# A plain fp32 query projection, early picks of two heads, and gate products one step later, in a one-core encoder layer with expert retrieval

## The chip, the cores and the metric

The kernel runs on one core of one Trainium2 chip. The metric is the device time in microseconds (us), the median of several runs. Names of engines: PE is TensorE (PEld its weight loads), DVE VectorE, ACT ScalarE, POOL GpSimd, SP the engine that issues most transfers.

## What is computed

One encoder layer for two sequences of 256 tokens (`x_prompt` and `x_sample`), width 1024: normalisation, input projection, a gated short convolution beside grouped-query attention, output projection, and then an expert retrieval in place of a feed-forward part. Only that last part matters here:

```python
q = (xf @ wq).reshape(T, 8, 2, 128)                  # 8 heads, two halves of 128
s = einsum('thpc,hpnc->thpn', q, subkeys)            # 128 key scores for each half
sv, si = top_k(s, 16)
cand = sv[..., 0, :, None] + sv[..., 1, None, :]     # 16 x 16 sums
cv, cp = top_k(cand, 16)
eidx = take_along_axis(si[0]*128 + si[1], cp)        # 16 experts of 16384, for each head
gates = softmax(cv)
a = gelu(einsum('thkd,td->thk', u_tab[eidx], x)) * gates
out = einsum('thk,thkd->td', a, v_tab[eidx])
```

## The kernel before

**Two ways to the experts.** The prompt's two tiles of 128 tokens *gather*: for each of 8 x 16 = 128 picks of a tile one indirect DMA from POOL (`g_issue`, L159) fetches one row of `uv` for each token, 128 rows of 8 KB, about 1 MB (`grow`); DVE forms the dot with `xg` (`g_dot`, L185), ACT the gelu and the gate (`g_weight`), DVE adds the weighted second half to `hg` (`g_val`). That is 256 gathers, through a ring of four tiles (`GBUF`, pool `ga`). The sample goes *densely*: every key row j of `u` (512 KB) is multiplied with all 256 tokens (the S loop, 128 steps, `pSj`, L880), times a dense gate matrix A, and A is then multiplied with every row of `v` (the V loop, 128 steps, `acc`, L908). A comes from one-hot matrices: for four tokens at a time `gates_dense` (L804) has DVE and ACT make `oi`, `oj`, `gh`, `gl` and PE multiply them (`pgm`, L855 and L856, eight products in fp16), 64 such steps.

**Order of the work.** The program is written in one stream, and a scheduler then orders each engine's instructions. First `front(0)` (prompt), then `projections` for the prompt (L742: eight heads in two halves each, `pqq`, and the key scores, `pn`), then the picks of tile 0 (`step0` while the heads go by; `fin0`, that is gates and decoding, after the last), `front(1)` (sample), `projections` for the sample, the S loop, the V loop. Work beside these is paced by credits: `bg(us)` after a piece of PE work adds `us` times a share to two accounts; whenever account a holds `GU` = 2.65, `gather()` handles one gather, and account b pays for steps of the tasks (tile 1's picks, later `gates_dense`). Picks enter `queue` when they are decoded; here all 128 of tile 0 after the last head (L753). In the V loop the gathers that are left are spread over 126 steps (L911). A gather's issue also waits for the PE instruction before it in the program (`pe_mark`), for its ring slot and for its index.

**Precision.** The prompt's projections run in a split form: `weights(..., split)` (L111) has ACT and DVE cut each weight tile into `whi` and `wlo` (in two tiles of the same ring `ga` as the gathers), `norm_T` cuts the activations (`xr` and `xrl`), and `mm` (L126) multiplies three terms in fp32r. The sample's run in plain fp32, where one call of the program is two PE instructions in the trace.

**Buffers.** Weights and `u`, `v` tiles go through four tiles of 512 KB (`wp`; the V loop has two more), loaded by SP. The S loop has four PSUM tiles for `pSj`, each freed by DVE's product with A (L885).

Of the kernel before, what the change touches and what calls it, by code (L numbers as in the profile page):

```python
# [18 lines left out]
P = 128  # L19
# [16 lines left out]
JH = 94  # L36
SF = 0.5
# [9 lines left out]
def encoder_layer(ctx: ExitStack, tc: tile.TileContext, xp, xs_, meta, vec, w_in, w_out, wq,  # L47
# [186 lines left out]
    def retrieval(pools, sv, si, cv, cp, gs, scores, t0, lkbuf, dc):  # L234
# [31 lines left out]
        def gates(t):  # L266
            ge_ = gate_all[:, t0 + t].rearrange("p (h k) -> p h k", k=KTOP)
            dve.tensor_tensor(ge_, cv[:, t], cv[:, t, :, 0:1].to_broadcast([P, PH, KTOP]), op=ALU.subtract)
            act.activation(gate_all[:, t0 + t], gate_all[:, t0 + t], AF.Exp)
            dve.tensor_reduce(gs[:, t], ge_, axis=AX.X, op=ALU.add)  # L270
            dve.reciprocal(gs[:, t], gs[:, t])
            dve.tensor_tensor(ge_, ge_, gs[:, t, :, None].to_broadcast([P, PH, KTOP]), op=ALU.mult)

        def lookup(mask, tab2, out):
            w = lkbuf(0)
            if tab2 is None:
                dve.tensor_tensor(w.rearrange("p h a k -> p h (a k)"), mask.rearrange("p h a k -> p h (a k)"),
                                  dc[:, 1:2].rearrange("p o a k -> p o (a k)").to_broadcast([P, PH, 256]), op=ALU.mult)
            else:
                dve.tensor_tensor(w.rearrange("p h a (k r) -> p (h a) k r", r=2),  # L280
                                  mask.rearrange("p h a (k r) -> p (h a) k r", r=2),
                                  tab2.rearrange("p h a r -> p (h a) r")[:, :, None, :].to_broadcast([P, PH * 16, 8, 2]),
                                  op=ALU.mult)
# [6 lines left out]
        def decode(t):  # L290
            s16 = t2.tile([P, 16, KTOP], F16, tag="s16", name="s16", bufs=1)
            dve.tensor_copy(s16, si[:, t])
            c16 = t2.tile([P, PH, KTOP], F16, tag="c16", name="c16", bufs=1)
            dve.tensor_copy(c16, cp[:, t])
            s4 = s16.rearrange("p (h q) k -> p h q k", q=2)
            di = t2.tile([P, PH, KTOP, 2], F16, tag="di", name="di", bufs=1)
            dj = t2.tile([P, PH, KTOP, 2], F16, tag="dj", name="dj", bufs=1)
            for r in range(2):
# [3 lines left out]
            mk = lkbuf(1)  # L302
            dve.tensor_tensor(mk, c16[:, :, None, :].to_broadcast([P, PH, 16, 16]),
                              dc[:, 0:1].to_broadcast([P, PH, 16, 16]), op=ALU.is_ge)
            lookup(mk, di, idx_i[:, t].rearrange("p (h k) -> p h k", k=KTOP))
            yield 6.0
            b16 = t2.tile([P, PH, KTOP], F16, tag="b16", name="b16", bufs=1)
            lookup(mk, None, b16)
            dve.tensor_tensor(b16, c16, b16, op=ALU.subtract)
            yield 4.0  # L310
            mk2 = lkbuf(1)
            dve.tensor_tensor(mk2, b16[:, :, None, :].to_broadcast([P, PH, 16, 16]),
                              dc[:, 2:3].to_broadcast([P, PH, 16, 16]), op=ALU.is_equal)
            lookup(mk2, dj, idx_j[:, t].rearrange("p (h k) -> p h k", k=KTOP))
            if t0 == 0:
                dve.scalar_tensor_tensor(eidx[:, t], idx_i[:, t], 128.0, idx_j[:, t], op0=ALU.mult, op1=ALU.add)
            yield 5.0
# [8 lines left out]
        def all_steps(tiles):  # L326
            for hd in range(PH):
                yield from head_steps(hd, tiles)
            for t in tiles:
                yield from fin_steps(t)  # L330

        def fin_steps(t):
            gates(t)
            yield 1.0
            yield from decode(t)

        return head_steps, fin_steps, all_steps

    def projections(xr, sk, scores, qp, step=None, split=False):
# [84 lines left out]
    def front(s, h):  # L424
# [275 lines left out]
        for t in range(2):  # L700
            tok = slice(t * P, (t + 1) * P)
            norm_T(lambda c: xr[:, c, tok], xs2[t], (lambda c: xrl[c.start // 4][:, :, tok]) if sp else None)
# [10 lines left out]
        if sp:  # L713
            return lambda c, k: xrl[c // 4][:, c % 4] if k else xr[:, c]
# [21 lines left out]
    heads0, fin0, _ = retrieval(r0t, *picks(r0p, "p0"), sc0, 0, lk0, dc0)  # L736
# [16 lines left out]
    queue.extend((0, k) for k in range(P))  # L753
# [33 lines left out]
    heads1, fin1, _ = retrieval(q1, *pk1, sc1, 2, lk1, dc1)  # L787
# [14 lines left out]
    tau = [0]  # L802

    def gates_dense():  # L804
# [13 lines left out]
        for t in range(2):  # L818
# [14 lines left out]
            yield 1.6  # L833
            for o in range(P // OC):
# [16 lines left out]
                for q in range(OC // 4):  # L851
                    pg = psg.tile([P, 4, P], F32, tag="g", name="pgm")
                    for r in range(4):
                        k = 4 * q + r
# [135 lines left out]
```

## Time and profile before

| | us |
|---|---|
| median of 3 runs | 1413.37 (1413.35 to 1417.03) |
| the profiled execution's own time | 1417.84 |
| its span | 1415.9 |
| PE, DVE, ACT, POOL busy | 94%, 72%, 33%, 31% of the span |

| stretch of the profiled span | us |
|---|---|
| `front(0)` | 0 to 143 |
| prompt's projections | 143 to 196 |
| `front(1)` | 196 to 345 |
| sample's projections | 345 to 416 |
| S loop | 416 to 950 |
| V loop | 950 to 1412 |

The profiled execution took 4.5 us more than the median; the span leaves out 1.9 us around it. Busy shares are averages over stretches with different limits, and a busy PE is not a PE at its peak, so the rows further down are taken by stretch.

### The profile page before, as it was taken

Reading aid. Unit: us, or ns where it says so; the run is one execution under the profiler, and the core shown is the slowest. Engines: PE = TensorE matmul, PEld = TensorE weight load, DVE = VectorE, ACT = ScalarE, POOL = GpSimd, SP = SyncE. Lnnn points to the kernel's source line nnn. Section 1 sums busy time; section 2 is a strip of 40 time slices with the busy share of each in tenths; the row PEclk is TensorE's granted clock in tenths of the full one; section 3 lists DMA queues with packets and bytes.
Section 4 is the critical chain, followed back from the end, with each engine's and each line's share of the span. In section 5 each row is a group of like instructions: output and inputs, shape, how many; then the busy total and the mean of one; then the engine's idle time right before and its main releaser. Section 6 shows DMA issues by size and latency. Waiting matters only on the chain. (4 is left out here: it accounts for less than half of the span.)

```text
span 1415.9 us, 17764 instructions
## 1 busy us (share of the span) xinstructions
PE 1329.3 (94%) x5868; PEld 925.7 (65%) x5868; DVE 1026.0 (72%) x2307; ACT 470.2 (33%) x1577; POOL 445.1 (31%) x481
## 2 busy tenths in 40 slices
PE   6998998998989987999999999899999999999998
PEld 5887996677868875788787787674433333344443
DVE  5656899775998876877887777576666666665665
ACT  4554433632222225777776311111111111111110
POOL 2101124331433221112121234243545545423331
PEclk9999999999999998999999999999999999999999
DMA  6434537578979997888988999899999999999997
GB/s 209 135 120 141 174 104 276 191 261 298 346 271 345 399 353 253 324 297 315 328 327 291 360 418 418 351 399 417 415 417 417 418 416 417 417 416 416 416 417 298
DMA packets 90235, 460.20 MB, mean 325 GB/s; under 512 B 10512, under 2 KB 11024, under 8 KB 57120
## 3 DMA queue, kind: packets, MB, share of 16 engines
q0 software_dynamic: 37296, 270.02, 48.2%
q1 hardware_dynamic: 50832, 182.33, 35.0%
q10 hardware_dynamic: 2016, 6.72, 1.3%
q8 instruction: 46, 0.75, 0.2%
q14 instruction: 45, 0.37, 0.1%
HBM read 454.81 MB, written 4.19 MB: 324 GB/s over the span
## 5 line engine op out<-in xcount | busy, mean ns | idle before, releaser
L159 POOL DMA_INDIRECT grow<-in_uv,eidx x256 | 366.3, 1431 | 701.4 <-DMA grow<-in_uv,eidx 174.0
L132 PE MATMUL pSj<-xr,u 128*128 128x256 f32 x2048 | 492.2, 392 | 21.0 <-DVE Ah L64 13.1
L132 PEld LDWEIGHTS pSj<-xr,u 128*128 128x128 f32 x2048 | 375.5, 193 | 85.3 <-DVE Ah L64 19.3
L64 DVE SCALAR_TENSOR_TENSOR grow<-grow,xg 128x1024 f32<-128x1024 f32 x256 | 312.7, 1222 | 158.1 <-DMA grow<-in_uv,eidx 150.4
L64 DVE SCALAR_TENSOR_TENSOR hg<-grow,aw,hg 128x1024 f32<-128x1024 f32 x256 | 328.4, 1283 | 89.7 <-ACT aw L64 88.2
L908 PE MATMUL acc<-v,Al 128*128 128x512 f32 x752 | 340.1, 601 | 4.9
L908 PEld LDWEIGHTS acc<-v,Al 128*128 128x128 f32 x752 | 137.3, 190 | 207.1 <-issue 146.1
L64 ACT ACTIVATE dots<-dots 128x1 f32<-128x1 f32 x256 | 51.6, 202 | 636.1 <-DVE grow L64 635.9
L908 PE MATMUL acc<-v,Ah 128*128 128x512 f32 x272 | 116.9, 592 | 0.0
L64 ACT ACTIVATE gl<-oj,gf 128x128 f16<-128x128 f16 x256 | 95.5, 393 | 9.7 <-DVE oj L64 9.4
L908 PEld LDWEIGHTS acc<-v,Ah 128*128 128x128 f32 x272 | 51.7, 190 | 65.1 <-issue 64.8
L64 ACT ACTIVATE aw<-dots,gate_all 128x1 f32<-128x1 f32 x256 | 74.8, 293 | 6.8
L64 DVE TENSOR_TENSOR wlo<-w,whi 128x1024 fp32r<-128x1024 f32 x42 | 51.1, 1218 | 19.2 <-ACT whi L64 13.2
L64 ACT ACTIVATE gh<-oj,gf 128x128 f16<-128x128 f16 x128 | 50.5, 394 | 27.5 <-DVE oj L64 27.2
L64 DVE TENSOR_TENSOR oj<-dup,io 128x512 f16<-128x512 f16 x64 | 27.1, 424 | 44.6 <-ACT gl L64 44.4
L132 PE MATMUL pqq<-xr,w 128*128 128x256 f32 x256 | 59.1, 385 | 0.0
L855 PE MATMUL pgm<-gh,oi 128*128 128x128 f16 x256 | 47.6, 220 | 11.3 <-ACT gh L64 11.3
L132 PEld LDWEIGHTS pqq<-xr,w 128*128 128x128 f32 x256 | 48.4, 194 | 6.4 <-ACT xr L64 0.2
L64 ACT ACTIVATE whi<-w 128x1024 fp32r<-128x1024 f32 x42 | 44.0, 1056 | 23.0 <-PE pqq L132 11.9
L856 PE MATMUL pgm<-gl,oi 128*128 128x128 f16 x256 | 49.0, 220 | 0.1
L132 PE MATMUL pc<-xT,w 128*128 128x258 f32 (+1 forms) x192 | 47.5, 390 | 1.1 <-DVE rb L64 0.6
L132 PEld LDWEIGHTS pc<-xT,w 128*128 128x128 f32 x192 | 34.9, 192 | 8.6 <-issue 2.5
(261 smaller groups left out, 1568.6 us busy)
## 6 DMA issues: line engine op xcount, KB each, us to landing
u<-in_u_t SPq DMA_DIRECT2D x128, 512.0 KB
v<-in_v_n SPq DMA_DIRECT2D x128, 512.0 KB
w<-in_w_in SPq DMA_DIRECT2D x36, 512.0 KB
w<-in_wq SPq DMA_DIRECT2D x32, 512.0 KB
w<-in_w_out SPq DMA_DIRECT2D x16, 512.0 KB
grow<-in_uv,eidx POOLq DMA_INDIRECT x256, 10.3
hdram<-h ACTq DMA_DIRECT2D x3, 512.0 KB
h<-in_xp SPq DMA_DIRECT2D x2, 512.0 KB
```

The source lines that it names most:

```text
L64: i = f(*a, **k)
L132: i = pe.matmul(out, st_(c, a), mv(c, b), start=(n == 0), stop=(n == NC * len(terms) - 1))
L159: i = pool.indirect_dma_start(out=r, out_offset=None, in_=uv, in_offset=bass.IndirectOffsetOnAxis(ap=eidx[:, t, k:k + 1], axis=0))
L855: pe.matmul(pg[:, r, :], oi[:, k, :], gh[:, k, :], start=True, stop=False)
L856: pe.matmul(pg[:, r, :], oi[:, k, :], gl[:, k, :], start=False, stop=True)
L908: i = pe.matmul(acc[t][q], A(j)[:, t * P:(t + 1) * P], vb[:, q * 512:(q + 1) * 512], start=j == 0, stop=j == P - 1, skip_group_check=True)
```

## The change

Three edits. `projections` of the prompt loses its split form: `w` is used as loaded, `xr` is fp32, `xrl` is gone. Decoding takes a range of heads, and `step0` decodes and queues the picks of heads 0 and 1 as soon as head 1 is chosen, the other six after head 7; from then on account a grows with the share `S0`. And `gates_dense` hands a step's products to `gate_unit` one step later.

```diff
+HPART = (2, PH)
+S0 = 0.4
...
-        def gates(t):
+        def gates(t, ha, hb):
...
-        def decode(t):
+        def decode(t, ha, hb):
+            n_h = hb - ha
...
+            mk = lkbuf(1)[:, :n_h]
...
             if t0 == 0:
-                dve.scalar_tensor_tensor(eidx[:, t], idx_i[:, t], 128.0, idx_j[:, t], op0=ALU.mult, op1=ALU.add)
+                dve.scalar_tensor_tensor(eidx[:, t, ks], idx_i[:, t, ks], 128.0, idx_j[:, t, ks], op0=ALU.mult, op1=ALU.add)
...
-            w = weights(wq, hd, split)
+            w = weights(wq, hd)
...
-                mm(pq, lambda c, k: w(c, k)[:, pp * P:(pp + 1) * P], xr, split=split)
+                mm(pq, lambda c, k: w(c)[:, pp * P:(pp + 1) * P], xr)
...
-        xr = gc.tile([P, NC, 256], F32R if sp else F32, tag="xr", name="xr")
-        if sp:
-            xrl = [r0t.tile([P, 4, 256], F32R, tag=f"lk{i}", name=f"xrl{i}", bufs=1) for i in range(2)]
+        xr = gc.tile([P, NC, 256], F32, tag="xr", name="xr")
...
     def step0(hd):
         for _ in heads0(hd, [0]):
             pass
-
-    projections(xr0, sk0, sc0, r0t, step0, True)
-    for _ in fin0(0):
-        pass
+        if hd + 1 in HPART:
+            ha = ([0] + list(HPART))[HPART.index(hd + 1)]
+            for _ in fin0(0, ha, hd + 1):
+                pass
+            if not ha:
+                credit["a"] = 0.0
+                share["a"] = S0
+            queue.extend((0, k) for k in range(ha * KTOP, (hd + 1) * KTOP))
+
+    projections(xr0, sk0, sc0, r0t, step0)
...
     tasks.append(tile1())
-    queue.extend((0, k) for k in range(P))
     share.update(a=SF, b=SB0)
...
+    def gate_unit(oi, gh, gl, a):
+        pg = psg.tile([P, 4, P], F32, tag="g", name="pgm")
+        for r in range(4):
+            pe.matmul(pg[:, r, :], oi[:, r, :], gh[:, r, :], start=True, stop=False)
+            pe.matmul(pg[:, r, :], oi[:, r, :], gl[:, r, :], start=False, stop=True)
...
+        tau[0] = a + 4
...
-                tau[0] = t * P + s0 + OC
+                due.append((oi, gh, gl, t * P + s0))
+                if len(due) > 1:
+                    gate_unit(*due.pop(0))
                 yield 1.1 + (4 * r_done[0] + 60) / 700
+            gate_unit(*due.pop(0))
```

POOL's queue at the first gathers (`cd` are the candidate sums of a head, `qst` belongs to `front`). Before:

```order
L258 TENSOR_TENSOR cd<-p0sv 128x3
L259 TENSOR_TENSOR cd<-p0sv 128x6
L106 TENSOR_TENSOR qst<-qst,mhalf 128x2 x2
L159 DMA grow<-in_uv,eidx 128x2048 x4
L106 TENSOR_TENSOR qst<-qst,mhalf 128x4 x2
```

After the change:

```order
L261 TENSOR_TENSOR cd<-p0sv 128x6
L264 TENSOR_TENSOR cd<-p0sv 128x8
L161 DMA grow<-in_uv,eidx 128x2048 x4
L260 TENSOR_TENSOR cd<-p0sv 128x16 x2
L260 TENSOR_TENSOR cd<-p0sv 128x8
```

The first four gathers stand among the candidate sums of the prompt's heads instead of behind `front(1)`'s first norms. Counted over the whole queue, 36 gathers stood before the first PE instruction of the S loop, 115 were tied to S steps and 105 to V steps; now it is 43, 116 and 97.

PE's queue at the first gate products, behind the three transposes that open `gates_dense`. Before:

```order
L823 MATMUL pg<-ident,gate_all 128x128
L132 MATMUL pSj<-xr,u 128x256 x11
L855 LDWEIGHTS oi
L855 MATMUL pgm<-gh,oi 128x128
L856 LDWEIGHTS oi
L856 MATMUL pgm<-gl,oi 128x128
L132 MATMUL pSj<-xr,u 128x256
L855 LDWEIGHTS oi
L855 MATMUL pgm<-gh,oi 128x128
```

After the change:

```order
L841 MATMUL pg<-ident,gate_all 128x128
L134 MATMUL pSj<-xr,u 128x256 x16
L809 LDWEIGHTS oi
L809 MATMUL pgm<-gh,oi 128x128
L810 LDWEIGHTS oi
L810 MATMUL pgm<-gl,oi 128x128
L809 LDWEIGHTS oi
L809 MATMUL pgm<-gh,oi 128x128
```

16 calls of the S loop stand ahead of the first product instead of 11, and the eight products of the step follow each other. Over the whole queue the 512 products stood in 222 unbroken runs between `pSj` calls, and now stand in 166.

ACT's queue in the prompt's projections (`qs` frees PE's PSUM tile of a half head). Before:

```order
L64 ACTIVATE qs<-pqq 128x256
L64 ACTIVATE sc_1571<-pn 128x256
L64 ACTIVATE whi<-w 128x1024
L64 ACTIVATE qs<-pqq 128x256
L64 ACTIVATE sc_1571<-pn 128x256
```

After the change, at the twelfth half head:

```order
L66 ACTIVATE sc_1565<-pn 128x256
L66 ACT_TABLE_LOAD
L66 ACTIVATE dots<-dots 128x1 x2
L66 ACTIVATE aw<-dots,gate_all 128x1 x2
L66 ACTIVATE qs<-pqq 128x256
```

The weight cuts are gone, and gelus of early gathers stand ahead of the copies that free PE's tiles.

## Rows read from the trace of the kernel before

**Rows 1.** The chain of work that ended last, pieces in order of time: start us, length us, what.
```profile
932.63 17.84 PE pSj L132 x80
950.47 44.65 PE acc L908 x104
...
1016.13 18.91 DMA v<-in_v_n
...
1267.60 144.48 PE acc L908 x336
```

**Rows 2.** Busy time by stretch: the stretch and its length, then for PE, PEld, DVE, ACT, POOL busy us and (x instructions), the granted clock, the DMA engines' share, GB/s.
```profile
143.00:196.30 53.30, 53.30 (x444) 53.27 (x444) 47.15 (x225) 24.61 (x46) 9.45 (x51) 0.97 0.50 153
196.30:345.00 148.70, 131.77 (x643) 104.05 (x642) 121.02 (x408) 59.52 (x156) 51.98 (x100) 0.97 0.67 240
...
545.60:800.00 254.40, 251.91 (x1472) 203.85 (x1470) 199.27 (x415) 178.71 (x715) 51.51 (x46) 1.00 0.86 310
800.00:950.20 150.20, 134.54 (x588) 112.39 (x587) 104.43 (x148) 27.32 (x108) 57.06 (x40) 0.97 0.97 393
950.20:1267.50 317.30, 312.44 (x690) 125.15 (x688) 209.06 (x251) 42.05 (x169) 147.85 (x82) 1.00 1.02 416
```

**Rows 3.** The same view for the gather tiles on POOL alone: busy us and (x gathers issued), then granted clock, DMA share, GB/s.
```profile
196.30:345.00 148.70, 23.59 (x20) 0.97 0.67 240
345.00:416.00 71.00, 13.66 (x12) 0.98 0.86 315
416.00:545.60 129.60, 32.81 (x27) 0.92 0.89 341
545.60:800.00 254.40, 51.51 (x46) 1.00 0.86 310
800.00:950.20 150.20, 55.33 (x37) 0.97 0.97 393
950.20:1267.50 317.30, 147.85 (x82) 1.00 1.02 416
```

**Rows 4.** The same view for the V loop's products (`acc`) on PE alone; eight instructions are one step.
```profile
950.20:1267.50 317.30, 312.33 (x688) 1.00 1.02 416
1267.50:1412.00 144.50, 144.43 (x337) 1.00 0.96 393
```

**Rows 5.** DMA queues from 1000 to 1200 us: packets, MB, share of the 16 engines (q0 carries POOL's transfers, q1 SP's); and the transfers issued.
```profile
q0 software_dynamic: 7607, 55.41, 66.9%
q1 hardware_dynamic: 7637, 27.81, 34.8%
...
v<-in_v_n SPq DMA_DIRECT2D x53, 512.0 KB
grow<-in_uv,eidx POOLq DMA_INDIRECT x53, 11.2
```

**Rows 6.** PE in order of time (start us, length us): the key scores after two following half heads in the prompt's projections (split), and a half head with the scores around it in the sample's (plain).
```profile
156.71 0.61 PE L346 MATMUL pn<-sk,qs 128*128 128x128 f32 x4
...
159.99 0.61 PE L346 MATMUL pn<-sk,qs 128*128 128x128 f32 x4
...
356.87 0.61 PE L346 MATMUL pn<-Ah,qs 128*128 128x128 f32 x4
357.31 3.62 PE L132 MATMUL pqq<-xr,w 128*128 128x256 f32 x16
360.77 0.61 PE L346 MATMUL pn<-Ah,qs 128*128 128x128 f32 x4
```

**Rows 7.** DVE in order of time ahead of the prompt's projections, and PE's first product there.
```profile
137.26 1.22 DVE L64 TENSOR_TENSOR wlo<-w,whi 128x1024 fp32r<-128x1024 f32 x1
...
139.13 0.68 DVE L64 TENSOR_TENSOR xrl<-pt,xr 128x512 fp32r<-128x512 f32 x1
139.88 1.28 DVE L64 SCALAR_TENSOR_TENSOR xs<-h,sst,gf 128x1024 f32<-128x1024 f32 x1
...
143.02 1.01 PE L132 MATMUL pqq<-xr,whi 128*128 128x256 f32 x3
143.82 0.50 PE L132 MATMUL pqq<-xrl,whi 128*128 128x256 f32 x1
```

**Rows 8.** PE in order of time around the first gate product, and further on in the gate steps (idle before, and what ended it, in brackets).
```profile
523.44 4.91 PE L132 MATMUL pSj<-xr,u 128*128 128x256 f32 x22
539.68 0.26 PE L855 MATMUL pgm<-gh,oi 128*128 128x128 f16 x1 [11.33 <-ACT gh L64]
...
645.14 0.65 PE L132 MATMUL pSj<-xr,u 128*128 128x256 f32 x2
645.63 0.22 PE L856 MATMUL pgm<-gl,oi 128*128 128x128 f16 x1
645.69 0.65 PE L132 MATMUL pSj<-xr,u 128*128 128x256 f32 x2
```

**Rows 9.** DVE in order of time at the same place.
```profile
536.09 1.22 DVE L64 SCALAR_TENSOR_TENSOR grow<-grow,xg 128x1024 f32<-128x1024 f32 x1 [2.19 <-DMA grow<-in_uv,eidx]
...
538.44 0.42 DVE L64 TENSOR_TENSOR oi<-dup,io 128x512 f16<-128x512 f16 x1
```

**Rows 10.** Waits: who waited for what, us in total, times, longest us. DVE from 143 to 345 us, PE from 345 to 416 us.
```profile
DVE grow L64 <- DMA grow<-in_uv,eidx: 11.0, 8, 3.0
...
PE pn L346 <- ACT qs L64: 6.7, 3, 4.7
```

More of the change, by code (lines that the diff above doesn't have):

```diff
@@ L288, in lookup @@
             dve.tensor_tensor(out, w[:, :, 0, :], w[:, :, 1, :], op=ALU.add)
[L290 to L294 removed]
+        def decode(t, ha, hb):
+            n_h = hb - ha
+            s16 = t2.tile([P, 16, KTOP], F16, tag="s16", name="s16", bufs=1)[:, :2 * n_h]
+            dve.tensor_copy(s16, si[:, t, 2 * ha:2 * hb])
+            c16 = t2.tile([P, PH, KTOP], F16, tag="c16", name="c16", bufs=1)[:, :n_h]
+            dve.tensor_copy(c16, cp[:, t, ha:hb])
             s4 = s16.rearrange("p (h q) k -> p h q k", q=2)
[L296 to L297 removed]
+            di = t2.tile([P, PH, KTOP, 2], F16, tag="di", name="di", bufs=1)[:, :n_h]
+            dj = t2.tile([P, PH, KTOP, 2], F16, tag="dj", name="dj", bufs=1)[:, :n_h]
             for r in range(2):
@@ L324, in head_steps, with fin_steps, projections @@
             yield 0.5 + 1.5 * len(tiles)
[L326 to L333, printed above, removed]
+        def fin_steps(t, ha=0, hb=PH):
+            gates(t, ha, hb)
             yield 1.0
-            yield from decode(t)
-        return head_steps, fin_steps, all_steps
-    def projections(xr, sk, scores, qp, step=None, split=False):
+            yield from decode(t, ha, hb)
+        return head_steps, fin_steps
+    def projections(xr, sk, scores, qp, step=None):
         late = []
@@ L701, in front @@
             tok = slice(t * P, (t + 1) * P)
-            norm_T(lambda c: xr[:, c, tok], xs2[t], (lambda c: xrl[c.start // 4][:, :, tok]) if sp else None)
+            norm_T(lambda c: xr[:, c, tok], xs2[t])
         hold[0] = False
@@ L734, in lk0 @@
         return r0t.tile([P, PH, 16, 16], F16, tag=f"lk{i}", name=f"lk{i}", bufs=1)
-    heads0, fin0, _ = retrieval(r0t, *picks(r0p, "p0"), sc0, 0, lk0, dc0)
+    heads0, fin0 = retrieval(r0t, *picks(r0p, "p0"), sc0, 0, lk0, dc0)
     def step0(hd):
@@ L802, in encoder_layer @@
     tau = [0]
+    def gate_unit(oi, gh, gl, a):
[3 more added lines that the diff above has]
+            pe.matmul(pg[:, r, :], oi[:, r, :], gl[:, r, :], start=False, stop=True)
+        n = r_done[0]
+        pj = pg.rearrange("p t j -> p j t")
+        for part, lo, hi in ((Al, 0, JH), (Ah, JH, P)):
+            m = min(max(n, lo), hi)
+            if m > lo:
+                av = part[:, 0:m - lo, a:a + 4]
+                dve.scalar_tensor_tensor(av, pj[:, lo:m], 1.0 / GSH, av, op0=ALU.mult, op1=ALU.mult)
+            if m < hi:
+                act.activation(part[:, m - lo:hi - lo, a:a + 4], pj[:, m:hi], AF.Copy, scale=1.0 / GSH)
+        tau[0] = a + 4
     def gates_dense():
@@ L833, in gates_dense @@
             yield 1.6
+            due = []
             for o in range(P // OC):
@@ L850, in gates_dense @@
                     act.activation(gl[:, q, :], oj[:, q, :], AF.Copy, scale=gf2[:, 1, s0 + q:s0 + q + 1])
[L851 to L854, printed above, removed]
-                        pe.matmul(pg[:, r, :], oi[:, k, :], gh[:, k, :], start=True, stop=False)
-                        pe.matmul(pg[:, r, :], oi[:, k, :], gl[:, k, :], start=False, stop=True)
-                    a = t * P + s0 + 4 * q
-                    n = r_done[0]
-                    pj = pg.rearrange("p t j -> p j t")
-                    for part, lo, hi in ((Al, 0, JH), (Ah, JH, P)):
-                        m = min(max(n, lo), hi)
-                        if m > lo:
-                            av = part[:, 0:m - lo, a:a + 4]
-                            dve.scalar_tensor_tensor(av, pj[:, lo:m], 1.0 / GSH, av, op0=ALU.mult, op1=ALU.mult)
-                        if m < hi:
-                            act.activation(part[:, m - lo:hi - lo, a:a + 4], pj[:, m:hi], AF.Copy, scale=1.0 / GSH)
-                tau[0] = t * P + s0 + OC
+                due.append((oi, gh, gl, t * P + s0))
+                if len(due) > 1:
+                    gate_unit(*due.pop(0))
                 yield 1.1 + (4 * r_done[0] + 60) / 700
+            gate_unit(*due.pop(0))
         ogx.close()
```

53 lines of the change are left out of this document (27 added, 26 removed).

## Prediction

> **What bounds the kernel now.** I read the chain of waits first, then busy time by stretch, then single stretches in order of time. The chain ends in the V loop: from 950 us PE alternates with `v` transfers of 18.9 us until 1267 us, and from there it is PE alone, 336 instructions in 144.48 us, 0.430 us each [rows 1]. So the V loop has two parts: in the first the DMA engines are the limit (share 1.02, 416 GB/s), in the second PE [rows 2, 4]. The first part takes 317.3 us for 688 instructions, which is 86 steps of 3.69 us; the second 144.5 us for 337, 42 steps of 3.44 us [rows 4]. The difference, 0.25 us for 86 steps, about 22 us, is what transfers cost PE there.
>
> Why the first part ends where it does: in it every `v` tile (0.5 MB) shares the engines with one gather (1 MB). From 1000 to 1200 us 53 of each were issued, and the two queues moved the same number of packets, 7637 and 7607, but 27.8 against 55.4 MB [rows 5]. Up to 950.2 us 20+12+27+46+37 = 142 gathers had been issued [rows 3]. The program puts 256-105 = 151 ahead of the V loop, so nine were overdue. While gathers are overdue they come as fast as the ring lets them, 82 in 317.3 us, one in 3.87 us [rows 3]; when they have caught up, the program's own pace holds them back and PE is the limit. In the program before, six of seven V steps carry a gather: 151+0.857x86 = 225 are due at 1267 us, and 142+82 = 224 have been issued. That closes.
>
> Ahead of the V loop: in the gate steps (546 to 800 us) PE is busy 251.9 of 254.4 us; in the S steps after them it is held back, 134.5 of 150.2 [rows 2]. In the prompt's projections PE is busy throughout, in `front(1)` 131.8 of 148.7 us [rows 2].
>
> **The change part by part.** The sum is made against the profiled execution, 1417.84 us, which lies 4.5 us above the median of 1413.37.
>
> *Start of the projections.* The cut of a weight tile (1.22 us) and two cuts of activations stand on DVE between the last `h` and the norm that yields `xs`; `xs` starts at 139.88 us, and PE then waits for `xrl` until 143.82 [rows 7]. Without them ACT's square and POOL's root remain in that chain; I estimate `xs` about 1.1 us earlier and 0.4 us for `xrl`: -1.5 us, bounds 0 and -2.6 (1.22 for the weight cut, twice 0.68 for `xrl` [rows 7]).
>
> *Plain fp32.* In the split form a half head takes 159.99-156.71 = 3.28 us, in plain fp32, as the sample's projections run, 360.77-356.87 = 3.90 us, PE busy throughout [rows 6]. 16 half heads: 16x0.62 = +9.9 us on PE. The floor is PE's own work; the ceiling adds ACT's late copies, which cost the sample's projections 6.7 us in three waits, 4.7 of them at the end [rows 10]: +9.9 to +12. DVE loses 16 weight cuts of 1.22 us and gains a few small instructions of a second decoding and the dots and sums of the early gathers; with two cuts fewer per head it has room under PE's 7.8 us. ACT and DVE are covered by PE as long as no `qs` copy waits.
>
> The Trainium skill, FP8 and Floating Point Precision, section TensorE Precision Notes, says that true fp32 takes four passes through the array. By that rule four passes stand against three terms, 4/3 of a half head's time, and not the 3.90/3.28 of the rows. It speaks against this edit; the trace shows the smaller price.
>
> *Early gathers.* The account grows by 0.4x3.9 = 1.56 for each half head, 0.59 of a gather, from head 1 on, and the ring takes four at once. By the order of the instructions seven more are issued before the S loop, one more in it, eight fewer in the V loop (97). They go past POOL's candidate sums, where one that waits for its ring slot holds up a later head's choice; PE does not wait for that choice, and 32 queued picks cover a late second decoding. SP's weight loads now wait for PE instead of for the cut; two heads' tiles lie ahead of it.
>
> What eight gathers fewer are worth in the V loop: I take nine overdue again, since the S steps that make them do not change. 159 are due at its start, 150 issued. The new pace is 100 gathers in 126 steps, 0.794. They catch up when 150+t/3.87 = 159+0.794t/3.69, that is 9/(0.2584-0.2152) = 208 us, 56.5 steps. The remaining 71.5 steps at 3.44 us are 246 us. In all 454 us instead of 317.3+144.5 = 461.8: **-7.8 us**. Bounds: nothing, if the head start is eaten up before the loop, and -20 us, if every byte counted (8x1.05 MB at 416 GB/s).
>
> *Gate products one step later.* PE now waits for its first product behind 16 calls instead of 11. It waited 11.33 us there [rows 8], because DVE came late: a gather's dot waited 2.19 us for its transfer, and the first `oi` started at 538.44 us [rows 9]. That order on DVE stays, so I take only what PE does meanwhile, five calls of two instructions of (360.77-357.31)/16 = 0.216 us [rows 6]: -2.2 us. Bounds: nothing, and -11.3 us if the whole wait went.
>
> *Longer runs of products.* A product between `pSj` calls costs more than itself: two `pSj` instructions and one product repeat every 645.69-645.14 = 0.55 us [rows 8], of which 0.43 us are the two and about 0.06 us the product, so 0.06 us is the change of kind. 56 runs fewer: -3.2 us, bounds 0 and -3.4, on a PE that is the limit of that stretch [rows 2]. What is late next there is PE's own work.
>
> `front(1)` is taken at 0: the same number of gathers fall into it, a shorter decoding stands at its start, and the bounds are -5 and +11 (below). The sum is -1.5+9.9-7.8-2.2-3.2 = **-4.8 us**: 1413.0 for a profiled execution, **1408.6 for the median**. About 0.3%, 4.2 us, is what a measurement of this kernel can tell from no change; the forecast lies just beyond it.
>
> **Rivals.**
>
> *The early stretch stalls (slower).* Gathers in the projections put dots and gelus that wait for transfers into the queues of DVE and ACT, ahead of copies and norms that PE needs. For it: PE already waited 17 us in all in `front(1)` (148.7-131.8) [rows 2], and eight dots waited 11.0 us for their transfers [rows 10]. Against it: the DMA engines are only half busy in the projections [rows 2], and DVE loses 16 cuts. Price: eight more such waits, 11 us, all on the path: -4.8+11 = +6.2, 1419.6 us. It decides from about 9 us lost between the first product and the S loop on.
>
> *The head start does not reach the V loop.* The S steps behind the gates run against the DMA engines too, share 0.97 [rows 2], and could leave more overdue. Then the -7.8 is missing: +3.0, 1416.4 us; and if the wait for the first gate product stays as well, so that two of three edits do nothing, 1418.6.
>
> *Every byte counts.* If `v` transfers got what gathers no longer take, the loop would come down by 20 us and not 7.8, 1396.4 us. Against it: the equal packets in the rows, which tie a `v` tile to one gather as long as any is overdue [rows 5].
>
> *Four passes.* If plain fp32 cost the prompt 4/3 of 3.28 us, 4.37 a half head, the projections would grow by 17.5 us and the time would be 1416.2 us; the sample's half head of 3.90 us speaks against it [rows 6]. It is the rule of the Trainium skill, FP8 and Floating Point Precision, section TensorE Precision Notes.
>
> **How the numbers follow.** Forecast 0.57, early stall 0.17, head start lost 0.14, every byte 0.10, four passes 0.02. The forecast's own range, from the bounds of its terms near the values taken, is 1402 to 1415; I put 0.35 of its 0.57 below 1409.1 and 0.22 within 0.3%. Faster: 0.35+0.10 = 0.45. Within: 0.22+0.12 of the lost head start+0.02 = 0.36. Slower: 0.17+0.02 = 0.19. The range 1399 to 1419.6 leaves out most of the case of every byte and the upper half of the stall.
>
> **What would show it.** In the changed profile: half heads of the prompt 3.90 us apart; the first gather near 171 us; the first `pSj` near 424 us (416-1.5+9.9); a wait of some 9 us before the first gate product; an S loop of 528 instead of 534 us; 150 gathers issued at its end; a V loop of 454 us whose DMA part ends after some 208 us. A first `pSj` later than 434 us shows the stall, a V loop of 442 us that every byte counts, one of 460 that the head start was lost. The prediction is wrong if the gain or loss comes from a stretch that this sum leaves at 0, `front(1)` above all.

## The result, and the profile after

| | before | changed |
|---|---|---|
| median of the runs on one chip, us | 1415.93 (7 runs) | 1423.58 (7 runs) |
| ratio to before, 95% interval | | 1.0063 [1.0042, 1.0084] |
| the profiled execution's own time | 1417.84 | 1423.44 |
| its span | 1415.9 | 1421.5 |

The change is slower, by 0.6%; the forecast was 0.3% faster. One run of all those in this document, of k4_split_early_sb, was disturbed; medians hold every run, ratios leave that one out. Busy time by stretch of the changed kernel, columns as in [rows 2]: the prompt's projections, `front(1)`, the sample's projections, then the S loop in three pieces and the V loop in two.

```profile
139.79:207.13 67.34, 66.50 (x338) 58.87 (x338) 49.95 (x261) 19.11 (x50) 21.48 (x61) 0.97 0.71 250
207.13:364.57 157.44, 134.03 (x621) 104.74 (x619) 124.02 (x410) 60.01 (x158) 63.78 (x99) 0.93 0.63 227
364.57:440.40 75.83, 66.31 (x322) 56.93 (x321) 66.08 (x314) 16.93 (x61) 30.46 (x55) 0.97 0.84 300
440.40:580.00 139.60, 125.61 (x581) 108.06 (x582) 112.90 (x278) 42.52 (x146) 40.50 (x43) 0.94 0.88 336
580.00:800.00 220.00, 219.33 (x1328) 181.53 (x1327) 180.80 (x383) 165.24 (x662) 49.49 (x41) 1.00 0.88 324
800.00:965.90 165.90, 151.16 (x660) 127.37 (x660) 115.23 (x162) 30.85 (x123) 60.47 (x45) 0.96 0.99 399
965.90:1149.60 183.70, 181.47 (x403) 72.98 (x402) 121.06 (x149) 24.96 (x100) 82.37 (x47) 1.00 1.02 416
1149.60:1417.40 267.80, 267.80 (x624) 118.38 (x624) 155.46 (x186) 30.32 (x122) 69.52 (x59) 1.00 0.97 385
```

The late part went as forecast: the S loop fell from 534 to 525.5 us (forecast 528), the V loop to 451.5 (forecast 454), and its DMA part ends after 184 us instead of 317 [rows 4]. The early part did not: the first `pSj` stands at 440.40 us, where the forecast had 424 and called 434 the sign of an early stall. To see which stretch lost it, here are the stages in us, each kernel cut at its own first instructions (before: `pqq` 143.0, `pkv` 198.9, second `pqq` 344.7, `pSj` 416.3, `acc` 950.3; the V loop counted to the end of the span). The four kernels of the first experiment are among them.

| | prompt's projections | `front(1)` | sample's projections | S loop | V loop |
|---|---|---|---|---|---|
| before | 55.9 | 145.8 | 71.6 | 534.0 | 465.6 |
| delayed products alone (e4_delay) | 55.9 | 145.2 | 71.8 | 533.7 | 457.3 |
| plain fp32 alone (e1_plain) | 66.2 | 144.5 | 74.7 | 531.9 | 464.9 |
| plain fp32, delayed products (e2_plain_delay) | 66.1 | 145.5 | 73.1 | 531.7 | 458.4 |
| plain fp32, early picks (e3_plain_early) | 67.6 | 157.2 | 75.8 | 534.5 | 457.0 |
| all three: the changed kernel | 67.3 | 157.5 | 75.8 | 525.8 | 455.3 |

In these six kernels `front(1)` is 12 us longer where there are early picks, and nowhere else. PE's waits of over 3 us there, in order of time (columns as in [rows 8]):

```profile
220.91 3.63 PE L134 MATMUL pq<-w,xT 128*128 128x256 f32 x10 [3.26 <-ACT v_sb L66]
...
283.60 1.74 PE L543 MATMUL psc<-kT,qT 64*128 64x272 f32 x4 [4.17 <-ACT pr L66]
...
338.34 20.35 PE L134 MATMUL po<-w,catT 128*128 128x256 f32 x86 [3.81 <-DVE catT L66]
```

The rows name ACT and DVE, but neither was at work on what PE wanted. The wait at 283.60 followed back: POOL in the 38 us ahead of it, the tile-1 candidate sums (`cd`) and the gathers.

```profile
245.07 0.93 POOL L161 DMA_INDIRECT grow<-in_uv,eidx  x1 [0.30 <-issue]
247.21 0.21 POOL L260 TENSOR_TENSOR cd<-p0sv 128x16 f32<-128x16 f32 x1 [1.21 <-DVE p0sv L66]
...
256.81 0.82 POOL L260 TENSOR_TENSOR cd<-p0sv 128x16 f32<-128x16 f32 x5 [5.42 <-DVE p0sv L66]
...
260.57 0.82 POOL L260 TENSOR_TENSOR cd<-p0sv 128x16 f32<-128x16 f32 x5 [2.61 <-DVE p0sv L66]
...
265.12 4.06 POOL L260 TENSOR_TENSOR cd<-p0sv 128x16 f32<-128x16 f32 x5 [1.06 <-DVE p0sv L66]
...
270.75 2.06 POOL L161 DMA_INDIRECT grow<-in_uv,eidx  x1 [0.17 <-DVE c L66]
273.12 0.95 POOL L161 DMA_INDIRECT grow<-in_uv,eidx  x1 [0.30 <-issue]
274.37 0.94 POOL L161 DMA_INDIRECT grow<-in_uv,eidx  x1 [0.31 <-issue]
```

For 24.75 us, from 246.00 to 270.75, POOL issues no gather; then three come at once. The DMA engines had little to do meanwhile (share 0.21 and 0.37 between 256 and 276 us). Two things held the first of the three. One is its ring slot: the ring has four tiles, and a gather can go out only when DVE has added the second half of the fourth one before it (`hg`). 14 of the 19 gathers in `front(1)` follow the end of that add by 0.76 to 1.7 us. Here the add ended at 266.79 us. ACT's weight for it was there at 251.56 us, but on DVE it stood behind a dot that waited for its own row and behind picks of tile 1 (DVE was busy all of 256 to 266 us):

```profile
254.77 1.22 DVE L66 SCALAR_TENSOR_TENSOR grow<-grow,xg 128x1024 f32<-128x1024 f32 x1 [3.08 <-DMA grow<-in_uv,eidx]
...
265.53 1.27 DVE L66 SCALAR_TENSOR_TENSOR hg<-grow,aw,hg 128x1024 f32<-128x1024 f32 x1
```

The other is POOL's own queue: the sums of tile 1's heads stand ahead of the gather and wait for DVE's picks, so that it goes out 3.96 us after the add and not 0.8. Of the 24.75 us some 3 are thus POOL's; the rest passes before the slot is free. Had only these 3 us been saved, the dot below would have waited some 1.8 us instead of 4.95 (an estimate, if nothing else moves). The longest wait for a row in `front(1)`, 5.3 us at 314.4 us, follows a gather that went out 0.78 us after its slot was free: there POOL's queue held nothing back. What the late row does to DVE, and then to ACT:

```profile
279.86 1.23 DVE L66 SCALAR_TENSOR_TENSOR grow<-grow,xg 128x1024 f32<-128x1024 f32 x1 [4.95 <-DMA grow<-in_uv,eidx]
```

```profile
281.13 0.20 ACT L66 ACTIVATE dots<-dots 128x1 f32<-128x1 f32 x1 [7.02 <-DVE grow L66]
281.37 0.29 ACT L66 ACTIVATE aw<-dots,gate_all 128x1 f32<-128x1 f32 x1
281.68 1.28 ACT L66 ACT_TABLE_LOAD   x1
282.97 0.49 ACT L66 ACTIVATE pr<-psc,sm 128x272 f32<-128x272 f32 x1
```

DVE's next dot waits 4.95 us for its row, ACT's gelu waits for that dot, behind the gelu stand a table load and the exponentials `pr`, and PE waits for these. And PE pays a second time. Busy time in stretches of 10 us from 270 us on (columns as in [rows 2]; the granted clock is the third number from the end):

```profile
270.00:280.00 10.00, 9.44 (x48) 6.98 (x47) 3.45 (x8) 1.75 (x4) 4.54 (x4) 1.00 0.76 279
280.00:290.00 10.00, 6.40 (x18) 4.24 (x18) 7.29 (x25) 5.29 (x16) 5.67 (x5) 0.67 0.54 205
290.00:300.00 10.00, 10.00 (x36) 6.50 (x36) 8.14 (x31) 5.92 (x14) 2.06 (x7) 0.82 0.53 199
300.00:310.00 10.00, 10.00 (x53) 8.10 (x51) 8.31 (x24) 4.48 (x12) 5.31 (x5) 1.00 0.70 238
```

In the stretch with the wait the granted clock falls to a mean of 0.67, and it stays at 0.82 in the next one although PE is busy all through: 36 instructions there, 53 in the one after (in steps of 2 us the clock is 0.50 from 284 to 292 and 1.00 from 294 us on). Over all of `front(1)` PE took 134.0 us for 621 instructions, against 128.9 for as many in the kernel before, whose clock was 0.97 and not 0.93. So of the 11.7 us some 6.5 are more waiting (23.4 for 16.9), and 5.2 more time for as many instructions, at the lower clock behind the waits.

### The profile page after: what moved, and what is told of

Its sections match the earlier page's. It is cut to its first block, busy times and chain, and to the rows that moved or that the text cites. A ratio compares the mean times of both kernels' runs of the same rounds, so it can differ in the third digit from the quotient of the medians.

```text
span 1421.5 us, 17473 instructions
## 1 busy us (share of the span) xinstructions
PE 1331.3 (94%) x5740; PEld 934.6 (66%) x5740; DVE 1006.2 (71%) x2317; ACT 457.1 (32%) x1564; POOL 439.7 (31%) x481
## 5 line engine op out<-in xcount | busy, mean ns | idle before, releaser
L161 POOL DMA_INDIRECT grow<-in_uv,eidx x256 | 344.9, 1347 | 708.6 <-PE acc L914 172.7
L134 PE MATMUL pSj<-xr,u 128*128 128x256 f32 x2048 | 483.4, 389 | 20.9 <-DVE Ah L66 14.1
L134 PEld LDWEIGHTS pSj<-xr,u 128*128 128x128 f32 x2048 | 380.3, 193 | 79.1 <-DVE Ah L66 18.3
L914 PE MATMUL acc<-v,Al 128*128 128x512 f32 x752 | 332.6, 597 | 2.2
L134 PE MATMUL pqq<-xr,w 128*128 128x256 f32 x512 | 120.1, 389 | 1.2 <-DMA w<-in_wq 1.2
L134 PEld LDWEIGHTS pqq<-xr,w 128*128 128x128 f32 x512 | 97.6, 196 | 15.1 <-DMA w<-in_wq 2.0
L66 ACT ACTIVATE aw<-dots,gate_all 128x1 f32<-128x1 f32 x256 | 74.7, 293 | 7.0
L809 PE MATMUL pgm<-gh,oi 128*128 128x128 f16 x256 | 45.0, 221 | 12.0 <-ACT gh L66 11.8
L66 ACT ACTIVATE gh<-oj,gf 128x128 f16<-128x128 f16 x128 | 50.0, 391 | 12.6 <-DVE oj L66 11.7
L810 PE MATMUL pgm<-gl,oi 128*128 128x128 f16 x256 | 45.7, 221 | 0.3
L66 DVE TENSOR_TENSOR wlo<-w,whi 128x1024 fp32r<-128x1024 f32 x26 | 31.6, 1220 | 18.6 <-ACT whi L66 12.8
L809 PEld LDWEIGHTS <-oi 128*128 128x128 f16 x256 | 25.2, 99 | 20.6 <-DVE oi L66 11.0
```

What stands on the lines that cost most here:

```text
L66: i = f(*a, **k)
L134: i = pe.matmul(out, st_(c, a), mv(c, b), start=(n == 0), stop=(n == NC * len(terms) - 1))
L161: i = pool.indirect_dma_start(out=r, out_offset=None, in_=uv, in_offset=bass.IndirectOffsetOnAxis(ap=eidx[:, t, k:k + 1], axis=0))
L809: pe.matmul(pg[:, r, :], oi[:, r, :], gh[:, r, :], start=True, stop=False)
L810: pe.matmul(pg[:, r, :], oi[:, r, :], gl[:, r, :], start=False, stop=True)
L914: i = pe.matmul(acc[t][q], A(j)[:, t * P:(t + 1) * P], vb[:, q * 512:(q + 1) * 512], start=j == 0, stop=j == P - 1, skip_group_check=True)
```

## The experiments

The ratio is to the kernel before on the same chip, with its 95% interval. "Delay" stands for the delayed gate products.

**1. The three edits apart (five rounds each).** Three of these kernels start from the changed one:

```diff
-HPART = (2, PH)                     # e1_plain, e2_plain_delay
+HPART = (PH,)
...
-                if len(due) > 1:    # e1_plain, e3_plain_early
+                if len(due) > 0:
```

The fourth, e4_delay, is the kernel before with `gate_unit` and `due` as in the change's diff.

> Only the plain fp32 projection of the prompt; picks decoded and queued after the last head, gate products not delayed. Theory A (the 16 us between the first projection product and the S loop come from gathers that are fetched early): front(1) and the sample's projections as before, 146 and 72 us; prompt's projections 67 us; start 3.2 us earlier; first pSj near 424.5; V loop 461; 1415.9-3.2+11.4 = 1424 us. Rival B (plain fp32 itself, by its later weight loads, disturbs front(1)): first pSj at 436 or later and a time of 1436 us or more.

> Plain fp32 and the delayed gate products, without early picks. Theory A: as the kernel with plain fp32 alone up to the first pSj (424.5), and 3 to 5 us less in the S loop, so about 1420 us. Rival B: first pSj at 436 or later, 1432 us. If the delayed products are worth nothing: 1424 us.

> Plain fp32 and the early picks, gate products not delayed. Theory A: front(1) near 157 us again, first pSj near 440, V loop near 452; 3 to 5 us above the changed kernel, 1427.5 us. Rival B: the same as the kernel with plain fp32 alone but for the 8 to 10 us saved in the V loop. If the delayed products are worth nothing: 1423.6 us.

> The kernel before with the delayed gate products alone. Theory (runs of products are longer, 222 to 166): first pSj at 416 as before, S loop 3 to 5 us shorter, V loop 462, so 1411 to 1413 us against 1415.9. Rival: the S loop is held by DVE or by transfers all the same, 1415.9 us.

Measured: e1_plain 1424.84 us, ratio 1.0062 [1.0042, 1.0082]; e2_plain_delay 1415.65, 1.0000 [0.9984, 1.0015]; e3_plain_early 1435.74, 1.0150 [1.0127, 1.0174]; e4_delay 1405.65, 0.9929 [0.9914, 0.9945]; before 1415.14. So plain fp32 costs 9.7 us, delay gives 9.5 (9.2 with plain fp32, 12.2 with all), and the early picks, expected to give 8, cost 10.9 (e3 against e1) or 7.9 (changed against e2). The first `pSj` stood at 425.2 and 426.8 us without early picks and at 442.8 with them: rival B is out. Of theory A these runs show that early picks lengthen `front(1)`, not yet that it is their fetches. Delay came out about twice as large as expected, which is why e2_plain_delay and e4_delay lie 4 to 7 us below the times expected of them, and e3_plain_early, which lacks it, 8 us above.

Where delay gives its time can be seen in e4_delay: first and last gate product mark the stretches (before, then e4_delay; columns as in [rows 2]).

```profile
539.70:788.20 248.50, 245.98 (x1436) 197.59 (x1436) 192.43 (x405) 178.96 (x714) 48.18 (x44) 0.99 0.85 305
788.20:950.30 162.10, 146.44 (x641) 122.72 (x641) 113.07 (x161) 30.60 (x122) 61.13 (x43) 0.97 0.98 392
```

```profile
538.50:771.30 232.80, 232.13 (x1395) 193.74 (x1395) 193.22 (x408) 180.00 (x713) 50.28 (x44) 0.98 0.89 321
771.30:947.10 175.80, 154.27 (x676) 131.16 (x674) 116.99 (x168) 32.12 (x128) 52.51 (x46) 0.94 0.97 384
```

The gate steps take 15.7 us less. By the instruction order 21 `pSj` calls fewer (440 for 461) stand between the first and the last product, 21x0.43 = 9.0 us, and the products are in 133 unbroken runs instead of 222, 89x0.06 = 5.3 us. The calls come back behind the gate steps, and the S loop is as long as before (533.7). But that part is limited by transfers, and in its longer time three more gathers are issued (43 for 40, counted one by one), so the V loop starts with 6 overdue instead of 9 and is 8.3 us shorter. By this reading PE time saved in the gate steps is paid out as DMA time.

**2. Early fetch, early decoding, and the number of gathers in `front(1)`.** f1_nofetch (five rounds), f2_phase and f3_load (three) are the changed kernel with one line each:

```diff
-S0 = 0.4                            # f1_nofetch
+S0 = 0.0
...
-SF = 0.5                            # f3_load
+SF = 0.4
...
+    credit["a"] += 1.3              # f2_phase, ahead of front(1)
     xr1 = front(1, hs1)
```

> The changed kernel with S0 = 0: the picks of heads 0 and 1 are decoded and queued early, but nothing is fetched before front(1). Theory A1 (the early fetches alone cost the 12 us of front(1)): front(1) 145 us, first pSj near 426, V loop near 458, 1415.7 us, as plain fp32 with delayed products. Rival A2 (the split decoding, with six heads' lookups at the start of front(1), crowds DVE): front(1) 150 us or more, 1421 us or more.

> The changed kernel with 1.3, half of GU, added to account a at the start of front(1): the same number of gathers, each half a gather's share earlier. Theory P (the long waits of front(1) come from where single dots fall against their transfers and against ACT's exponentials): front(1) differs from 157.5 by over 3 us, either way. Rival L (the load of more dots and sums on DVE): 156 to 159 us again. By the order, the gate products now stand in 57 unbroken runs instead of 165, with as many pSj calls between the first and the last as without early picks: at 0.06 us for a run the gate steps should take 6.5 us less, 227 instead of 234 us.

> The changed kernel with SF = 0.4 instead of 0.5: some 15 gathers are issued in front(1) instead of 19, about as many dots as in the kernel before. Rival L (load): front(1) 147 us or less, time near 1415 (10 us less there, 2 us more in the V loop, where 101 gathers are left instead of 97). Theory P (places of single dots): anything from 145 to 157, with DVE's waits for transfers, not the count of dots, in step with PE's waits.

Measured: f1_nofetch 1408.92, 0.9946 [0.9930, 0.9963]; f2_phase 1418.77, 1.0015 [0.9989, 1.0042]; f3_load 1408.06, 0.9945 [0.9924, 0.9967]; before 1416.85. What they did to `front(1)`, with DVE's busy time and DVE's waits for gathered rows in it:

| | `front(1)` | DVE busy | DVE waits for rows | PE waits | clock |
|---|---|---|---|---|---|
| before | 145.8 | 118.7 | 11.0 | 16.9 | 0.97 |
| e2_plain_delay | 145.5 | 118.5 | 9.6 | 15.8 | 0.96 |
| changed | 157.5 | 124.0 | 17.1 | 23.4 | 0.93 |
| f1_nofetch | 138.0 | 116.4 | 7.0 | 11.8 | 0.98 |
| f2_phase | 160.3 | 130.1 | 13.5 | 23.0 | 0.92 |
| f3_load | 144.8 | 117.3 | 11.0 | 15.5 | 0.96 |

The early decoding is not the cost: without the fetches `front(1)` is 7.5 us shorter than with no early decoding at all, better than A1 had expected, and A2 is out. The fetches are the cost. f2_phase decided nothing between P and L (2.8 us, just under its bound; and it issued 21 gathers in `front(1)`, not 19, so the load was not held). Its gate steps, 230.8 us in 57 runs, gave 3.1 of the 6.5 us expected: PE was busy 6.0 us less in them (227.2 for 233.2), but waited 3 us more. f3_load came out as L said, three gathers fewer and 12.7 us less (and 7 us below L's time), but work and waits fell together. In every row the stretch is DVE's work plus its waits plus 14.6 to 17.4 us. That made me expect DVE's work to be what counts (theory D), and the next two tested it.

**3. Work or waits.** One run each, with its profile.

```diff
-SB0 = 0.35                          # h4_lesspicks, on the changed kernel
+SB0 = 0.15
...
             bg(3.0)                 # h1_dve, on e2_plain_delay
+            if s == 1:
+                for _ in range(2):
+                    z = tmp.tile([P, 1024], F16, tag="z", name="z", bufs=1)
+                    dve.tensor_tensor(z, h[:, t, :], h[:, t, :], op=ALU.mult)
```

> The kernel with plain fp32 and delayed products, without early picks, and with eight products on VectorE added in front(1) that nothing reads (128x1024, two in each of four pieces; about 1.2 us each by the like operations of the traces). It adds work to the computation and takes none away. Theory D (front(1) is as long as DVE's work and its waits for transfers, plus some 16 us, in all seven profiles so far): front(1) 145.5+8x1.2 = 155 us. Rival (PE's own chain through ACT sets it, and DVE has slack): 148 us or less.

> The changed kernel with SB0 = 0.15 instead of 0.35: less of the picking of tile 1 is done on DVE in front(1), and more after it; the gathers in front(1) are the same. Theory D: front(1) gets shorter by as much as DVE's busy time and waits for transfers there do, and stands again 16 us above their sum; what is moved comes back after front(1). Rival (the gathers alone make it long): 156 to 159 us.

h1_dve took 1413.8 us and settles nothing: nothing held the added products back, and the scheduler put them into the prompt's projections. There DVE was busy 45.99 us with 234 instructions (37.92 with 227 in e2_plain_delay), in `front(1)` no longer than before (118.9), which took 145.9 us.

h4_lesspicks took 1404.04 us, and `front(1)` fell to 142.6, though not as I had expected: DVE's work there stayed (124.1 and 124.3 us, 410 instructions in both), with the same 19 gathers. Only the waits went (and the stretch is 14.8 us above work and waits), from

```profile
DVE grow L66 <- DMA grow<-in_uv,eidx: 17.1, 7, 5.3
```

to (columns as in [rows 10])

```profile
DVE grow L66 <- DMA grow<-in_uv,eidx: 3.5, 2, 2.7
```

A lower SB0 lets tile 1's steps come later in the program, so fewer candidate sums stand ahead of gathers on POOL, and fewer picks ahead of dots and adds on DVE. It also leaves a debt in account b that starts the gate steps later (344 `pSj` calls ahead of the first product instead of 248, 58 runs instead of 165). The next two take these apart.

**4. The order in `front(1)` alone, the debt alone (five rounds each).** On the changed kernel:

```diff
-SB0 = 0.35                          # k1_sb
+SB0 = 0.15
...
     run_tasks()
+    credit["b"] = -17.68            # k1_sb; the value of the changed kernel
+    credit["b"] = -39.12            # k2_debt (SB0 as it was)
```

> The changed kernel with SB0 = 0.15 in front(1), and account b set afterwards to what the changed kernel has there (-17.68), so that the gate steps start at the same call of the S loop as in the changed kernel (248 calls ahead of the first product, 165 runs): only the order in front(1) differs. Theory W (the dots' waits for transfers, late because POOL issues gathers behind tile 1's candidate sums, made front(1) long): front(1) near 142.6 with DVE's work unchanged (124 us), S loop 526, 1408.7 us. Rival G (the gain of the run with SB0 = 0.15 came from its later gate steps): 1419 us.

> The changed kernel with account b set to -39.12 after front(1), the value that SB0 = 0.15 leaves: front(1) as changed, the gate steps start after 344 calls instead of 248 and have 58 runs of products instead of 165. Theory W: front(1) 157.5 again, S loop 4 to 5 us shorter, 1419 us. Rival G: 1405 to 1410 us.

Measured: k1_sb 1409.57, 0.9944 [0.9924, 0.9963]; k2_debt 1420.50, 1.0021 [1.0001, 1.0041]; before 1416.07. Both as theory W said. `front(1)` took 141.8 us in k1_sb and 156.7 in k2_debt, the S loop 526.7 and 522.8. POOL in k1_sb at the place shown above (gathers and sums), and DVE's add that frees the slot of the gather at 262.62:

```profile
245.87 1.20 POOL L161 DMA_INDIRECT grow<-in_uv,eidx  x1 [3.29 <-DVE rb L66]
...
259.40 0.82 POOL L260 TENSOR_TENSOR cd<-p0sv 128x16 f32<-128x16 f32 x5
...
262.62 1.28 POOL L161 DMA_INDIRECT grow<-in_uv,eidx  x1 [2.08 <-PE ptp L561]
264.95 1.46 POOL L161 DMA_INDIRECT grow<-in_uv,eidx  x1 [1.05 <-DVE p0cv L66]
266.72 1.06 POOL L161 DMA_INDIRECT grow<-in_uv,eidx  x1 [0.30 <-issue]
...
271.63 1.00 POOL L161 DMA_INDIRECT grow<-in_uv,eidx  x1 [0.19 <-issue]
```

```profile
260.58 1.27 DVE L66 SCALAR_TENSOR_TENSOR hg<-grow,aw,hg 128x1024 f32<-128x1024 f32 x1
```

15.6 us without a gather instead of 24.75: the gather goes out 0.77 us after its slot is free, and the slot comes back earlier. From dot to the end of the add it takes 9.1 us here and 13.5 in the changed kernel (mean of the first fifteen gathers issued in `front(1)`). And the whole of `front(1)` has 2.6 us of waits for rows:

```profile
DVE grow L66 <- DMA grow<-in_uv,eidx: 2.6, 2, 2.0
```

PE's longest wait is now 3.3 us, on `v_sb`; those on `pr` and `catT` of 4.2 and 3.8 us are gone, the clock is 0.96, and the same work on DVE fits into 15.7 us less. With one number changed, and account b put back, the changed kernel goes from 1.0063 to 0.9944. The run moves tile 1's picks on DVE and its sums on POOL together; which of the two queues gives how much no run shows. Theory W names POOL's queue alone; the ring slots show DVE's in it too.

**5. Versions.** f4_ss64 and k3_delay_sb are e4_delay with one number changed (`SS = 0.64`; `SB0 = 0.15`). b1_split_early has split projections, HPART = (2, PH) with S0 = 0, delay and SS = 0.64; b2_split_early_sf has SF = 0.4 besides; k4_split_early_sb has SS = 0.60 and SB0 = 0.15 instead. Five rounds each.

```diff
+        if early[0]:                # b1, b2, k4: the split form uses lk0, lk1 for xrl
+            return r0t.tile([P, 2, 16, 16], F16, tag=f"le{i}", name=f"le{i}", bufs=1)
         return r0t.tile([P, PH, 16, 16], F16, tag=f"lk{i}", name=f"lk{i}", bufs=1)
```

> The kernel before with the delayed gate products and SS = 0.64 instead of 0.60: 120 gathers are tied to S steps instead of 115, 100 to V steps instead of 105. Theory: the gate steps have DMA room (share 0.89), about three more gathers are issued in them, 149 at the start of the V loop against 156 due; 7 overdue caught up at 0.2584-0.794/3.69 = 0.0432 per us are 162 us at 0.068 lost per us, 11 us against 13 with 5 overdue at 0.0261: 2 us less, 1403.7. Rival: DVE, or the transfers, hold the S loop longer for each added gather, 1406 to 1410.

> A version put together from the runs: split projections as before, two heads decoded early in buffers of their own but nothing fetched early (S0 = 0), delayed products, SS = 0.64. Theory: the 7 us that early decoding took off front(1) come on top of 1403: 1396 us. Rival: in the split projections DVE is busy 49.5 of 55.8 us, and 4.4 us of decoding there delay the cuts that PE waits for: 1400 us or more.

> The same version with SF = 0.4 as well: 15 or 16 gathers issued in front(1) instead of 20. Theory D: front(1) 8 us shorter for some 8 us less of dots, sums and waits on DVE; four more overdue gathers in the V loop cost about 6 us: 1394 to 1396 us. Rival: DVE is no longer the limit of front(1) after the early decoding, 1400 us.

> The kernel before with delayed products and SB0 = 0.15. Theory W applies to the kernel before too, whose dots waited 10.7 us for transfers in front(1): waits 3 to 5 us, front(1) 138 to 140 us instead of 145.2, and an S loop 4 us shorter for 58 runs; 1405.65-6-4 = 1396 us. Rival (the waits there have another cause than POOL's order): front(1) 144 us or more, 1402 us.

> The version with split projections, two heads decoded early, nothing fetched early and delayed products, with SB0 = 0.15 (SS = 0.60): front(1) was 143.8 with 9.8 us of waits; theory W: 137 to 139 us, S loop 4 us shorter than 530; 1402-6-4+2 = 1394 us. Rival: no change in front(1), 1401 us.

| | median | ratio to before | `front(1)` | S loop | V loop |
|---|---|---|---|---|---|
| f4_ss64 | 1403.01 | 0.9924 [0.9897, 0.9950] | 145.4 | 530.9 | 454.0 |
| b1_split_early | 1401.98 | 0.9909 [0.9887, 0.9931] | 143.8 | 529.2 | 454.5 |
| b2_split_early_sf | 1401.29 | 0.9910 [0.9886, 0.9933] | 140.4 | 530.7 | 458.5 |
| k3_delay_sb | 1410.38 | 0.9968 [0.9950, 0.9985] | 144.9 | 522.4 | 468.2 |
| k4_split_early_sb | 1406.71 | 0.9911 [0.9877, 0.9945] | | | |

No stages are read for k4_split_early_sb. Its time lies above both that were expected of it, 1394 and 1401 us.

f4_ss64 met its 1403.7. b1 and b2 went by their rivals. In b1 the early decoding gave 1.6 us in `front(1)` and not 7: beside split projections DVE has less room for it, as the rival had it (busy 51.5 of 56.5 us in the projections, 42.3 of 66.3 in f1_nofetch). b2 gained 3.4 us in `front(1)` and lost 4 in the V loop. k3 went by its rival: without early fetches `front(1)` kept its 10.8 us of waits with SB0 = 0.15, so the place of tile 1's steps accounts for the changed kernel's extra waits, not for those that were there before. What causes these stays open, but in the main it is not POOL's queue: 14 of the 16 gathers of k3's `front(1)` that need a slot freed go out 0.76 to 1.3 us after it is free. Its time is 8 us above even the rival's, as the V loop (109 gathers tied to its steps) was 11 us longer than e4_delay's. b1 and b2 beat both kernels, but their intervals overlap with those of k4_split_early_sb, f4_ss64 and e4_delay: beyond the delayed products no gain is shown.

## Why the prediction was wrong

**The step that failed** is "`front(1)` is taken at 0", on the ground that the same number of gathers falls into it. The number was right (19 for 20), and the time 12 us more. It matters what order they stand in: with the ring full from the start, dots, adds and gelus follow from the first piece on, among the picks and sums of tile 1, and each later gather waits for an earlier one's add. DVE's waits for rows there are 17.1 us instead of 11.0. The change's early picks were called worth -7.8; they cost 8 to 11. f1_nofetch (`front(1)` 138.0 us without early fetches) and k1_sb against the changed kernel (14 us by the medians, 1.0063 to 0.9944 by the ratios, with the same fetches) show that early fetches and the place of tile 1's steps make the loss together. How it is shared between DVE's queue, which frees the slots, and POOL's stays open.

- *The rival "early stretch stalls"* named the mechanism, dots that wait for transfers ahead of copies that PE needs, and its bound of 11 us in `front(1)` was met (11.7 in the stage table), in part by luck: not eight more waits of dots but seven instead of eight, 6.1 us longer in all, and 5.2 us of PE at a lower clock, which it had not counted. Its place, in the prompt's projections too, was wrong: there PE waits 0.83 us, for weights. That it got 0.17 was the error of weighing. Against it stood that DMA was half busy; but the transfers were late because they were issued late, and that row could not speak to it.
- *Plain fp32*: forecast +9.9, measured 10.3 (66.2 for 55.9 us), half heads 3.90 us apart as forecast:

```profile
148.60 0.61 PE L347 MATMUL pn<-sk,qs 128*128 128x128 f32 x4
...
152.50 0.61 PE L347 MATMUL pn<-sk,qs 128*128 128x128 f32 x4
...
190.77 1.99 PE L134 MATMUL pqq<-xr,w 128*128 128x256 f32 x8 [0.83 <-DMA w<-in_wq]
```

  The Trainium skill, FP8 and Floating Point Precision, section TensorE Precision Notes, gives true fp32 four passes; the 4.37 us a half head worked out from that rule is not what the trace shows. That working scaled the whole half head, the key scores' 0.44 us included, and took a pass to be as long in either form; by the rows a term of the split form is (3.28-0.44)/24 = 0.118 us and a plain call 0.43.
- *Start of the projections*: forecast -1.5, nothing that can be told. PE did not wait for `xrl` until 143.82, as the prediction read it: its first product stood at 143.02, and the one with `xrl` followed without a wait [rows 7]. The first `pqq` stands at 140.4 to 143.1 us in the seven profiles with split projections and at 139.8 to 142.4 in the eleven with plain ones.
- *The V loop*: the rule held within 3 us. Of 159 gathers due 151 had been issued; 8/0.0432 = 185 us (the DMA part took 184) at 0.068 lost per us are 13 us above 128x3.44 = 440 and 4 us of tail, 457, measured 455.3. For e4_delay (6 overdue; the expectation of f4_ss64 has 5) it gives 460, measured 457.3; before (9) 468, measured 465.6. It was 4 us short for k3_delay_sb: 7 overdue, 464 by the rule, 468.2 measured. The two loops together are 9.0 us shorter in the changed kernel than in e2_plain_delay (5.9 in the S loop, 3.1 in the V loop), 7.8 forecast, all in the V loop. But without delay (e3_plain_early against e1_plain) the S loop is 2.6 us longer and the V loop 7.9 shorter, so how much of this the head start gives stays open.
- *Delayed products*: forecast -5.4, measured -9.5. The wait for the first product, forecast to fall to some 9 us, is still 11.42 us. Five more calls are done ahead of it in the same 123.5 us, but at a clock of 0.96 for 0.94; in e4_delay, at 0.94, they take 1.7 us more (125.1). So that term (-2.2) is not shown. Two are mis-sized: 0.06 us for a run holds, but e4_delay has 89 fewer and not 56, and the `pSj` calls that move behind the gate steps, counted at nothing, turned into DMA time as far as the rows of experiment 1 show.

```profile
545.38 7.07 PE L134 MATMUL pSj<-xr,u 128*128 128x256 f32 x32
563.87 0.27 PE L809 MATMUL pgm<-gh,oi 128*128 128x128 f16 x1 [11.42 <-ACT gh L66]
```

- *The sample's projections*, also left at 0, took 4.2 us more. Early picks are a part of it at most: e1_plain, without them, has 74.7 us, 3.1 more than before. The wait of 3.76 us ahead of the first `pSj`, which the kernels without early picks do not have, stands in place of one of 4.7 us that they have at the last `pn` [rows 10]:

```profile
440.40 5.84 PE L134 MATMUL pSj<-xr,u 128*128 128x256 f32 x18 [3.76 <-ACT Ah L66]
```

Forecast terms were -1.5+9.9-7.8-5.4 = -4.8. Measured by the runs apart: about +9.7 for plain fp32, +8 for early picks in the presence of the rest, -9.5 for delay, +8 in all; the changed kernel is 7.65 above.

## What to carry to other kernels

When a prefetch is moved forward, follow each transfer round its whole loop: what frees its buffer, on which queue that stands, and what stands ahead of the issue itself. What matters is not how many transfers fall into a stretch but what holds each of them, since a consumer that waits in its queue holds up what stands behind it, here also the add that frees the next buffer. Time edits apart before judging their sum: here one edit's 9.5 us was hidden under two that cost 10 and 8. And where two stretches have different limits, time that one engine saves in the first may be worth more in the second as transfer time than it looks.

## Not expected of the hardware

A wait of PE costs more than itself: the four `psc` at 283.60 us took 1.74 us behind the 4.17 us wait, four of the same form 0.73 at full clock; the mean of 0.67 in that stretch is a mix of the two levels, 1.2 and 2.4 GHz (0.50 and 1.00 in the steps of 2 us).

```profile
235.25 0.73 PE L543 MATMUL psc<-kT,qT 64*128 64x272 f32 x4
```

Five candidate sums on POOL took 4.06 us at 265.12 and 0.82 at 260.57. Beside the slow ones DVE ran dots and sums of 128x1024 almost without a break from 265.53 to 271.8 us; beside the fast ones it was busy too, with small operations. The Trainium skill, Trainium Architecture — The Big Picture, section What this means for kernel authors, says that DVE and POOL share a port pair under an exclusive lock; the rows agree, and no run here tested it.

Of the program rather than the chip: edits far ahead of the gate steps left their delayed products in 57, 133, 143 or 165 unbroken runs (f2_phase, e2_plain_delay, f3_load, changed; 166 where other products count as a break too), so the S loop can move by some microseconds with edits that have nothing to do with it.
